# SiLU gate on one core: tiles of 8 rows with two output buffers and a last store in pieces

## The chip, the cores and the metric

The kernel runs on one core of a Trainium2 chip. A core has a matrix engine (not used here), VectorE (DVE), ScalarE (ACT), GpSimd (POOL) and SyncE (SP), an on-chip memory of 128 partitions (SBUF), and 16 DMA engines that move data between SBUF and the chip's main memory (HBM). Here SP issues the loads and ACT the stores; each of the two has a DMA queue of its own, and both queues are served by the same 16 DMA engines. The metric is device time in microseconds (us), the median of several runs; lower is better.

## The reference

The input has 32 x 512 = 16,384 rows of 2,048 floats. The first half of a row goes through SiLU and is multiplied by the second half.

```python
def reference(x: np.ndarray) -> np.ndarray:
    half_dim = x.shape[-1] // 2
    x1, x2 = (x[..., :half_dim].copy(), x[..., half_dim:].copy())
    silu_x1 = x1 * (1 / (1 + np.exp(-x1)))
    return (silu_x1 * x2).astype(np.float32)
```

So 134.2 MB are read and 67.1 MB are written, and nothing is used twice.

## The kernel before

The rows are cut into tiles. A tile with K rows per partition takes 128 x K consecutive rows of the input; partition p holds rows pK to pK+K-1, so each partition is filled from one contiguous run of K x 8 KiB and gives back one contiguous run of K x 4 KiB. The plan (lines 34 to 50) is one tile with K = 4, twenty with K = 6, and one with K = 4: 22 tiles.

The loop at line 54 goes over the tiles in order. For each it takes an input buffer `xt` from `in_pool` (2 buffers of 48 KiB per partition), issues the load on SP (line 59), takes an output buffer `ot` from `out_pool` (4 buffers of 24 KiB), and then works through the tile in pieces of KC = 2 rows: ACT computes SiLU of the first halves into `ot` (line 64), DVE multiplies `ot` in place by the second halves (line 69). When all pieces are done, ACT issues one store of the whole tile (line 74).

The order of work follows from the queues and the buffers. SP holds only loads; the load of tile i+2 waits until DVE has read tile i, since it takes the same buffer. ACT's queue is: the tile's activations, then its store, which waits for DVE's last multiplication, then the next tile's activations. The first activation of a tile waits for the load, and for the store that last used its `ot` buffer (four tiles back). The framework inserts these waits.

Of the kernel before, what the change touches and what calls it, by code (L numbers as in the profile page):

```python
# [1 line left out]

# [4 lines left out]


@with_exitstack
def kernel(  # L10
    ctx: ExitStack,
    tc: tile.TileContext,
    x: bass.AP,
    out: bass.AP,
):
    nc = tc.nc
    P = nc.NUM_PARTITIONS

    x_flat = x.flatten_outer_dims()
    out_flat = out.flatten_outer_dims()  # L20

    num_rows, in_cols = x_flat.shape
    half = in_cols // 2
    dt = x_flat.dtype

    K_MAIN = 6
    K_EDGE = 4
    KC = 2

    in_pool = ctx.enter_context(tc.tile_pool(name="in_pool", bufs=2))  # L30
    out_pool = ctx.enter_context(tc.tile_pool(name="out_pool", bufs=4))

    rows_per_part_total = num_rows // P
    rem = rows_per_part_total - 2 * K_EDGE
    if rem > 0 and rem % K_MAIN == 0:
        plan_k = [K_EDGE] + [K_MAIN] * (rem // K_MAIN) + [K_EDGE]
    else:
        plan_k = []
        rem = rows_per_part_total
        while rem > 0:  # L40
            k = min(K_MAIN, rem)
            plan_k.append(k)
            rem -= k

    plan = []
    row = 0
    for k in plan_k:
        plan.append((row, k))
        row += P * k
    assert row == num_rows  # L50

    KT = max(K_MAIN, K_EDGE)

    for bi, (row0, K) in enumerate(plan):
        xv = x_flat[row0:row0 + P * K].rearrange("(p k) d -> p k d", k=K)
        ov = out_flat[row0:row0 + P * K].rearrange("(p k) d -> p k d", k=K)

        xt = in_pool.tile([P, KT, in_cols], dt, name="xt")
        nc.sync.dma_start(out=xt[:, :K, :], in_=xv)  # L59

        ot = out_pool.tile([P, KT, half], dt, name="ot")
        for c in range(0, K, KC):
            ce = min(c + KC, K)
            nc.scalar.activation(  # L64
                out=ot[:, c:ce, :],
                in_=xt[:, c:ce, :half],
                func=mybir.ActivationFunctionType.Silu,
            )
            nc.vector.tensor_mul(  # L69
                out=ot[:, c:ce, :],  # L70
                in0=ot[:, c:ce, :],
                in1=xt[:, c:ce, half:],
            )
        nc.scalar.dma_start(out=ov, in_=ot[:, :K, :])


# [1 line left out]
_INS = ['x']  # L78
_OUTS = [((32, 512, 1024), 'float32')]


# [23 lines left out]
```

## Time and profile before

| | |
|---|---|
| median of 3 runs | 474.58 us (474.44 to 474.65) |
| span of the profiled execution | 473.1 us |
| ACT activation, 128x2048 | x64, mean 1899 ns |
| DVE multiplication, 128x2048 | x64, mean 2287 ns |
| load of 6 rows per partition | 6144 KB, 34.8 us from issue to landing |
| store of 6 rows per partition | 3072 KB, 27.8 us from issue to landing |
| load / store of 4 rows per partition | 20.7 / 15.4 us from issue to landing |

The span runs from the first to the last instruction of the profiled execution; the measured time also holds what lies around it. Engine rows give the busy time and its share of the span. A digit row cuts the span into 40 equal slices and gives the busy share of each in tenths. For the DMA queues the page gives packets, megabytes and the time that the packets took as a share of 16 engines' span; q1 is the queue of SP's loads, q10 that of ACT's stores. "Landing" is the moment when a DMA's completion reaches the waiting engine.

### The profile page before, as it was taken

To read this page: it belongs to the slowest core of one execution; us is meant where nothing else is said; L and a number is where in the kernel's file an instruction comes from. 1 tells how busy PE (TensorE), PEld (TensorE's weight loads), DVE (VectorE), ACT (ScalarE), POOL (GpSimd) and SP (SyncE) were. 2 spreads that over 40 slices of the span, in tenths; PEclk is the share of its full clock that TensorE was granted. 3 is DMA by queue.
4 is the path that set the end of the run, shared out by engine and by line. 5 is a ranking of instruction groups with operands and counts; after the bars stand their busy time and mean duration, and the time that the engine had idled before them with its cause. 6 is when DMAs were issued, how large, how long until landed. Compare 5 with 4: busy or idle time off the path is not lost.

```text
span 473.1 us, 296 instructions
## 1 busy us (share of the span) xinstructions
DVE 142.9 (30%) x64; ACT 118.9 (25%) x65; POOL 0.2 (0%) x4
## 2 busy tenths in 40 slices
DVE  0323505050514324050505142231505050513323
ACT  1340404041231404040413214040404042231411
POOL 0000000000000000000000000000000000000000
DMA  8999999999999999999999999999999999999995
GB/s 355 449 398 424 432 430 455 420 428 451 414 432 441 432 443 432 416 434 447 426 428 457 418 435 436 443 432 424 432 443 418 438 453 411 451 432 418 433 420 244
DMA packets 6338, 201.35 MB, mean 426 GB/s; under 512 B 704, under 2 KB 704, under 8 KB 704
## 3 DMA queue, kind: packets, MB, share of 16 engines
q1 hardware_dynamic: 3168, 134.22, 65.9%
q10 hardware_dynamic: 3168, 67.11, 33.0%
q14 instruction: 2, 0.02, 0.0%
HBM read 134.22 MB, written 67.11 MB: 426 GB/s over the span
## 4 chain that ended last, share of the span: by engine, by line
DMA 78%; DVE 14%; ACT 4%; issue 1%; DVEq 0%; SPq 0%; ACTq 0%
DMA xt<-in_x_dram 78%; DVE ot L69 14%; ACT ot L64 4%; DVEq L100 0%; SPq L59 0%; ACTq L64 0%
## 5 line engine op out<-in xcount | busy, mean ns | idle before, releaser
L69 DVE TENSOR_TENSOR ot<-ot,xt 128x2048 f32<-128x2048 f32 x64 | 142.9, 2287 | 322.8 <-ACT ot L64 322.8
L64 ACT ACTIVATE ot<-xt 128x2048 f32<-128x2048 f32 x64 | 117.6, 1899 | 343.4 <-DMA xt<-in_x_dram 343.4
L64 ACT ACT_TABLE_LOAD x1 | 1.3, 1283 | 0.7 <-PEq L89 0.7
L89 POOL MEMSET const-bfloat16-1.0<- 128x1 bf16 x1 | 0.1, 103 | 0.0
L89 POOL MEMSET const-uint8-127<- 128x1 uint8 x1 | 0.1, 103 | 0.0
L89 POOL MEMSET const-float32-1.0<- 128x1 f32 x1 | 0.1, 100 | 0.0
L89 POOL MEMSET const-float32-0.0<- 128x1 f32 x1 | 0.1, 99 | 0.2 <-issue 0.2
## 6 DMA issues: line engine op xcount, KB each, us to landing
xt<-in_x_dram SPq DMA_DIRECT2D x20, 6144.0 KB, 34.8
out_dram<-ot ACTq DMA_DIRECT2D x20, 3072.0 KB, 27.8
xt<-in_x_dram SPq DMA_DIRECT2D x2, 4096.0 KB, 20.7
out_dram<-ot ACTq DMA_DIRECT2D x2, 2048.0 KB, 15.4
```

The source lines that it names most:

```text
L64: nc.scalar.activation(out=ot[:, c:ce, :], in_=xt[:, c:ce, :half], func=mybir.ActivationFunctionType.Silu,)
L69: nc.vector.tensor_mul(out=ot[:, c:ce, :], in0=ot[:, c:ce, :], in1=xt[:, c:ce, half:],)
L89: nc = _bacc.Bacc("TRN2", target_bir_lowering=False, num_devices=1)
```

## The change

Every tile has 8 rows per partition: 16 equal tiles, loads of 64 KiB per partition and stores of 32 KiB. The input pool keeps two buffers (now of 64 KiB), the output pool has two (of 32 KiB) instead of four, so the SBUF in use is 192 KiB per partition in both kernels. The first two loads are issued ahead of the loop, and the load of tile i+2 is issued at the end of tile i. Of the last tile each piece of 2 rows is stored on its own, right after its multiplication in the program's text. The chunk size of the compute stays at 2 rows, SP issues the loads and ACT the stores as before.

```diff
-    K_MAIN = 6
-    K_EDGE = 4
+    K = 8
     KC = 2
+    n_tiles = num_rows // (P * K)
+    assert n_tiles * P * K == num_rows
 
     in_pool = ctx.enter_context(tc.tile_pool(name="in_pool", bufs=2))
-    out_pool = ctx.enter_context(tc.tile_pool(name="out_pool", bufs=4))
+    out_pool = ctx.enter_context(tc.tile_pool(name="out_pool", bufs=2))
...
+    xv = x_flat.rearrange("(n p k) d -> n p k d", p=P, k=K)
+    ov = out_flat.rearrange("(n p k) d -> n p k d", p=P, k=K)
...
+    def load(i):
+        xt = in_pool.tile([P, K, in_cols], dt, name="xt")
+        nc.sync.dma_start(out=xt, in_=xv[i])
+        loaded[i] = xt
...
+    load(0)
+    load(1)
+    for i in range(n_tiles):
+        xt = loaded.pop(i)
+        last = i == n_tiles - 1
+        ot = out_pool.tile([P, K, half], dt, name="ot")
         for c in range(0, K, KC):
-            ce = min(c + KC, K)
+            ce = c + KC
...
+            if last:
+                nc.scalar.dma_start(out=ov[i][:, c:ce, :], in_=ot[:, c:ce, :])
-        nc.scalar.dma_start(out=ov, in_=ot[:, :K, :])
+        if not last:
+            nc.scalar.dma_start(out=ov[i], in_=ot)
+        if i + 2 < n_tiles:
+            load(i + 2)
```

More of the change, by code (lines that the diff above doesn't have):

```diff
@@ L24 @@
     dt = x_flat.dtype
-    K_MAIN = 6
-    K_EDGE = 4
+    K = 8
     KC = 2
+    n_tiles = num_rows // (P * K)
+    assert n_tiles * P * K == num_rows
     in_pool = ctx.enter_context(tc.tile_pool(name="in_pool", bufs=2))
-    out_pool = ctx.enter_context(tc.tile_pool(name="out_pool", bufs=4))
[L33 to L61, printed above, removed]
+    out_pool = ctx.enter_context(tc.tile_pool(name="out_pool", bufs=2))
+    xv = x_flat.rearrange("(n p k) d -> n p k d", p=P, k=K)
+    ov = out_flat.rearrange("(n p k) d -> n p k d", p=P, k=K)
+    loaded = {}
+    def load(i):
[8 more added lines that the diff above has]
+        ot = out_pool.tile([P, K, half], dt, name="ot")
         for c in range(0, K, KC):
-            ce = min(c + KC, K)
+            ce = c + KC
             nc.scalar.activation(
```

## The prediction

> **What bounds the kernel now.** I read the busy shares first, then the DMA queues, then the waits, then the chain, and last the windows at the end of the span. From the page:
>
> ```profile
> span 473.1 us, 296 instructions
> DVE 142.9 (30%) x64; ACT 118.9 (25%) x65; POOL 0.2 (0%) x4
> DMA  8999999999999999999999999999999999999995
> q1 hardware_dynamic: 3168, 134.22, 65.9%
> q10 hardware_dynamic: 3168, 67.11, 33.0%
> HBM read 134.22 MB, written 67.11 MB: 426 GB/s over the span
> ```
>
> No compute engine reaches a third. The 16 DMA engines are 9 tenths or more busy in every slice but the first and the last; loads (q1) and stores (q10) together fill 98.9% of them. So the time is bytes over rate, plus what the engines stand idle at both ends. The waits say the same: ACT waits for loads in every tile, and no row has it waiting for a store.
>
> ```profile
> ACT ot L64 <- DMA xt<-in_x_dram: 343.4, 22, 16.8
> DVE ot L69 <- ACT ot L64: 322.8, 22, 15.6
> ```
>
> The chain of waits shows the cadence: two tiles from 116.28 to 159.88 us, 43.55 on average, so 21.77 us for a tile of 6 rows (6.29 MB in, 3.15 MB out): 433.5 GB/s. The end, by timeline and then by windows (columns: stretch, length, busy DVE, ACT and POOL, clock, DMA share, GB/s):
>
> ```profile
> 459.29 3.71 ACT L64 ACTIVATE ot<-xt 128x2048 f32<-128x2048 f32 x2 [10.47 <-DMA xt<-in_x_dram]
> 461.23 4.49 DVE L69 TENSOR_TENSOR ot<-ot,xt 128x2048 f32<-128x2048 f32 x2 [9.29 <-ACT ot L64]
> 465.76 0.34 ACTq L74 DMA_DIRECT2D out_dram<-ot  x1
> ```
> ```profile
> 462.00:463.00 1.00, 1.00 (x1) 0.99 (x1) 0.00 (x0) 1.00 0.97 418
> 463.00:464.00 1.00, 1.00 (x2) 0.00 (x0) 0.00 (x0) 1.00 0.12 49
> 464.00:465.00 1.00, 1.00 (x1) 0.00 (x0) 0.00 (x0) 1.00 0.00 0
> 465.00:466.00 1.00, 0.72 (x1) 0.00 (x0) 0.00 (x0) 1.00 0.00 0
> 466.00:467.00 1.00, 0.00 (x0) 0.00 (x0) 0.00 (x0) 1.00 0.62 262
> ```
>
> The last load lands at 459.26; the engines finish the older store at about 463.1 (3.85 us of backlog), then stand idle until about 466.4, since the last store waits for the whole tile. That hole of 3.3 us is the only one that a schedule of this kind can win back. After it come 4.8 us of store and 1.9 us to the end of the span (471.2 to 473.1).
>
> **What the Trainium skill says.** "DMA: Bandwidth & Descriptors", Where 436 GB/s comes from: 16 SBUF ports give 435 GB/s. The trace agrees, 433.5: only 0.4% is left for a better stream. The same page, Queues, rings and completion order: each DMA engine takes turns between the queues packet by packet. The page of the profile fits: 3168 packets are 22 DMAs x 144, that is 16 engines x (8 runs + 1 semaphore), so one run of one partition, 48 KiB or 24 KiB, is one packet, and with both queues filled the bytes go 2 to 1. The same page, Latency and other measured facts: HBM rows at a pitch of 512 KiB gave 207 GB/s where 214 is full, 3% less, and larger powers of two far less. No run here shows such a pitch; I use it for a rival.
>
> **The change part by part.**
>
> Unit: one 8-row load is 8.39 MB / 433.5 = 19.35 us of all engines, one store 9.68, one cycle 29.0.
>
> Issues. SP has 16 instead of 22 issues of 0.33 us, ACT 19 instead of 22 of 0.36, beside full queues: 0. Loads are issued at the end of tile i instead of the start of tile i+2, but SP carries nothing else and waits for the same thing, DVE's last read of tile i. Cost 0.
>
> Load slack. A 6-row tile takes 8.65 us from first activation to store issue (443.31 to 451.97), an 8-row tile one more multiplication, 11.0. The load of i+2 is issued 11.0 after load i landed, while load i+1 needs 29.0: 18 us of slack (13 before). Cost 0; without that cover each microsecond late would be paid 16 times.
>
> Output buffers 4 to 2. The activation of tile i newly waits for store i-2. Replay, with T(i) the landing of load i: load 1 runs alone until store 0 starts at T(0)+12.0 (11.0 and about 1 us to start), has 7.35 left, gets two thirds, so T(1) = T(0)+23.0; store 0 has moved 3.68 and has 6.0 left, done at T(1)+18. From there both queues are always filled, so T(i+1) = T(i)+29.0, and store i-2 lands at about T(i)-10. Behind a late wait stand ACT's whole queue and then DVE, but the 18 us above cover that too. Cost 0. The old kernel replayed likewise (6-row load 14.5, store 7.25, stores issued 8.65 after a landing): store 1 starts 9.7 after T(1), load 2 lands at T(1)+18.9 with 3.05 of store 1 moved, and 4.2 is left; that backlog is carried on to the last landing. Measured there: 3.85. So I trust the replay to about half a microsecond.
>
> Packets. A run grows to 64 and 32 KiB; packets fall by a quarter. If all of the 0.4% under the ceiling were per packet, a quarter of 1.8 us returns: 0 to -0.45. I take 0, because the ceiling itself may not be exact.
>
> Start. First compute moves from 13.1 to about 22.8, but load 1 is queued behind load 0: engines stay busy. The first two slices miss little more than start-up. Cost 0; bounds -0.5 to +0.5, since a dip at 24 to 28 us, when the first store joins, is unexplained.
>
> End. At T(15) store 14 has 6.0 left. In the built program ACT's order for the last tile is three activations, three stores, the fourth activation, the fourth store. ACT is free at T(15)+5.5 (three activations, 5.51), piece 0 is issued then and its bytes start 0.6 later, as before (465.76 to 466.4): 6.1, just as the backlog ends: 0.1 idle. Each piece is 2.42 us. Pieces 1 and 2 are issued at 6.5 and 8.8 and queue behind piece 0: busy to 13.4. The fourth activation is held behind piece 2's store and its wait for DVE: 9.2 to 11.1, multiplication to 13.4, issue at 13.4, bytes from 14.05: 0.7 idle. Last bytes at 16.5, end of span 1.9 later, T(15)+18.4.
>
> Sum: bytes equal, idle at the end 0.8 instead of 3.3: -2.5. A quarter of a microsecond is taken off for the doubt in the backlog (if it ends 1 us sooner, idle is 1.8 and the gain 1.5): -2.3. Span 470.8. The profiled run's own whole time is not given; the median 474.58 lies 1.5 above its span, and I leave that as it is: 472.3 us.
>
> **The rivals.**
>
> Slower by the stream's rate: partition starts in HBM now lie 64 KiB apart for loads and 32 KiB for stores, powers of two, where 48 and 24 were not, and engines that run in step might meet in the same part of HBM. The place is the 440 us of steady cadence; it decides from 0.5% on (2.3 of 464). Bounds 0 (the old stream is at the ceiling) and 3% (the skill's 512 KiB row, 14 us). An estimate between, 0.8%, is +3.7, less 2.3: 476.0. Against it: the old kernel's last load has a pitch of 32 KiB, and while it runs the rate is no lower:
>
> ```profile
> 445.00:450.00 5.00, 4.75 (x3) 3.81 (x3) 0.00 (x0) 1.00 1.02 441
> 450.00:455.00 5.00, 1.94 (x1) 0.00 (x0) 0.00 (x0) 1.00 1.08 465
> 455.00:459.00 4.00, 0.00 (x0) 0.00 (x0) 0.00 (x0) 1.00 0.93 401
> ```
>
> Slower by arbitration: if a run of 64 KiB goes as two packets of 32, turns are one to one and stores drain at half the rate instead of a third. Then T(1) = T(0)+26.7 with 2.3 of store 0 left, store 1 is all out by T(2) = T(1)+31.4, and so on in turn; T(15) finds 2.3 of backlog, the engines idle from there to 6.1, and 0.7 later: 4.5 against 3.3, +1.2, 475.8. For it: no run of 64 KiB has been seen here. Against: 48 KiB goes as one.
>
> No change: the backlog at T(15) is some 2 us shorter than replayed (stores favoured when the first joins): idle from T(15)+4.0 to 6.1 and 0.7 later, 2.8 instead of 3.3, -0.5, and the dip at the start grows by 0.2 with the larger first tile: 474.3.
>
> Faster still: packets give their 0.45 and the backlog covers the whole start of the pieces: 471.6. It belongs to the forecast's own range.
>
> **How the numbers follow.** Forecast (end hole filled) 0.60, own range 471.4 to 473.5, all of it faster; no change 0.13; rate 0.15, slower; arbitration 0.12, of which two thirds are slower by over 0.2% (0.95 us, what a measurement here can tell from no change) and one third not. Faster 0.60, same 0.17, slower 0.23. The range: the forecast's low end to the rate rival's middle, 471.3 to 476.0, which leaves out half of the rate case and a little of the forecast.
>
> **What would show it.** Right: a cadence of 29.0 us, DMA share 1.0 and 433 GB/s in the middle, no idle microsecond after the last load but one of about 0.7 before the fourth piece, and 18.4 us from the last load's landing to the end. Packets: 144 for each load; 272 would speak for arbitration, and idle engines from 2 to 6 us after the last landing with it. A cadence of 29.2 or more would speak for the rate. A row in which ACT waits for a store would show the buffers to be short. If the span falls though the hole stays, my account of the end is wrong.

## The result and the profile after

| | before | after |
|---|---|---|
| median | 474.55 us (474.44 to 474.65, 4 runs) | 471.88 us (471.59 to 472.29, 4 runs) |
| ratio | | 0.9943, 95% interval 0.9928 to 0.9957 |
| span of the profiled execution | 473.1 us | 470.1 us |
| landing of the last load | 459.29 us | 452.05 us |
| from there to the end of the span | 13.8 us | 18.05 us |

The changed kernel is 2.7 us faster. The two spans differ by 3.0, since the profiled execution of the kernel before was a little slower than its median: in every run for which both are known, the time is 1.7 to 1.8 us above the span, so a span of 473.1 belongs to a run of about 474.9. The page of the changed kernel:

```profile
span 470.1 us, 267 instructions
DVE 142.4 (30%) x64; ACT 118.3 (25%) x65; POOL 0.2 (0%) x4
DMA  8999999999999999999999999999999999999998
q1 hardware_dynamic: 2304, 134.22, 66.2%
q10 hardware_dynamic: 2736, 67.11, 33.1%
out_dram<-ot ACTq DMA_DIRECT2D x15, 4096.0 KB, 39.7
```

Compare the digit row with that of before: nothing differs but the last slice, 8 instead of 5. The loads' packets are 2304 / 16 = 144 for each load, so a run of 64 KiB went as one packet. Between the second and the last landing (the first activation of each tile in the timeline; 45.89 and 452.05 below) 14 tiles take 406.2 us, 29.0 each, and 12.58 MB in 29.0 us is 434 GB/s, the rate of before to within about a tenth of a percent. That tenth turns out to count; it is taken up in the section on the prediction.

The waits of the changed kernel (who waited for whom; us in total, times, longest):

```profile
ACT ot L56 <- DMA xt<-in_x_dram: 340.4, 16, 21.9
DVE ot L61 <- ACT ot L56: 322.9, 17, 24.7
ACT ot L56 <- DVE ot L61: 3.5, 1, 3.5
```

No row has ACT waiting for a store: two output buffers are enough. The third row is new. It is the last tile's fourth activation, held behind the third piece's store. Two parts of the timeline, the second landing and the end (start, duration, engine, what):

```profile
45.89 5.51 ACT L56 ACTIVATE ot<-xt 128x2048 f32<-128x2048 f32 x3 [15.84 <-DMA xt<-in_x_dram]
...
452.05 5.51 ACT L56 ACTIVATE ot<-xt 128x2048 f32<-128x2048 f32 x3 [21.65 <-DMA xt<-in_x_dram]
456.32 4.74 ACTq L67 DMA_DIRECT2D out_dram<-ot  x3
461.11 1.91 ACT L56 ACTIVATE ot<-xt 128x2048 f32<-128x2048 f32 x1 [3.54 <-DVE ot L61]
465.37 0.34 ACTq L67 DMA_DIRECT2D out_dram<-ot  x1
```

And by windows of it (stretch, length, busy DVE, ACT, POOL, clock, DMA share, GB/s):

```profile
448.00:449.00 1.00, 0.00 (x0) 0.00 (x0) 0.00 (x0) 1.00 0.00 0
...
457.00:458.00 1.00, 1.00 (x1) 0.56 (x1) 0.00 (x0) 1.00 0.54 229
458.00:459.00 1.00, 1.00 (x2) 0.00 (x0) 0.00 (x0) 1.00 0.93 393
...
464.00:465.00 1.00, 1.00 (x1) 0.00 (x0) 0.00 (x0) 1.00 0.95 401
465.00:466.00 1.00, 0.34 (x1) 0.00 (x0) 0.00 (x0) 1.00 0.24 98
466.00:467.00 1.00, 0.00 (x0) 0.00 (x0) 0.00 (x0) 1.00 0.94 393
```

The last two columns need care. The view books a packet, with all its bytes and its whole duration, in the window in which the packet starts. A packet of 32 KiB lasts 1.2 us here and one of 64 KiB 2.4 us, so a single microsecond can show too little or too much: the window at 448 shows nothing at all, though all 16 engines were busy through it. Where this text says "by packets", the figure is therefore worked out from the start and the duration of every packet in the trace, as a mean over the 16 engines.

By packets, the engines stood idle for 3.3 us between the older store and the last one in the kernel before. Now the older store ends 6.0 us after the last landing and each engine goes straight on to the first piece; the thin window at 457 is only such an effect of booking. One hole is left, before the fourth piece: 0.9 us by packets, 0.8 by the windows.

### The profile page after: what moved, and what is told of

Read it like the earlier page. It is cut to its first block, busy times and chain, and to the rows that moved or that the text cites. A ratio compares the mean times of both kernels' runs of the same rounds, so it can differ in the third digit from the quotient of the medians.

```text
span 470.1 us, 267 instructions
## 1 busy us (share of the span) xinstructions
DVE 142.4 (30%) x64; ACT 118.3 (25%) x65; POOL 0.2 (0%) x4
## 3 DMA queue, kind: packets, MB, share of 16 engines
q1 hardware_dynamic: 2304, 134.22, 66.2%
## 4 chain that ended last, share of the span: by engine, by line
DMA 80%; DVE 15%; ACT 4%; issue 0%; ACTq 0%; SPq 0%
DMA xt<-in_x_dram 80%; DVE ot L61 15%; ACT ot L56 4%; SPq L45 0%; ACTq L67 0%; ACTq L56 0%
## 6 DMA issues: line engine op xcount, KB each, us to landing
out_dram<-ot ACTq DMA_DIRECT2D x15, 4096.0 KB, 39.7
```

## The experiments

Each was timed beside the kernel before, on the same chip; that kernel's median was 474.55 or 474.56 each time, as in the table above, so the experiments can be set beside the changed kernel's 471.88 as well.

**1. The last store in pieces, on the old tiles.**

```diff
-        nc.scalar.dma_start(out=ov, in_=ot[:, :K, :])
+            if bi == len(plan) - 1:
+                nc.scalar.dma_start(out=ov[:, c:ce, :], in_=ot[:, c:ce, :])
+        if bi < len(plan) - 1:
+            nc.scalar.dma_start(out=ov, in_=ot[:, :K, :])
```

> The old tiles of 4, 6 and 6 rows; only the last store goes in two pieces of 2 rows. Theory of the end hole: the backlog ends 3.85 us after the last landing, the first piece's bytes start at 4.85, the second queues behind it; the idle engines shrink from 3.3 to about 1.0 us, so 2.3 us faster than before: 472.3. Theory of the stream (the gain comes from larger runs and fewer packets): as before, 474.5.

Measured: 472.42 us (472.35 to 472.54, 5 runs), ratio 0.9955 (0.9943 to 0.9967). Windows:

```profile
462.00:463.00 1.00, 1.00 (x1) 0.67 (x1) 0.00 (x0) 1.00 0.91 393
463.00:464.00 1.00, 1.00 (x2) 0.00 (x0) 0.00 (x0) 1.00 0.07 25
464.00:465.00 1.00, 1.00 (x1) 0.00 (x0) 0.00 (x0) 1.00 0.94 393
```

One thin microsecond where there were 3.3 of idle time (0.8 by packets). Pieces alone, on the old tiles, bring 2.1 of the 2.7 us.

**2. The new tiles with the last store whole.**

```diff
-            if last:
-                nc.scalar.dma_start(out=ov[i][:, c:ce, :], in_=ot[:, c:ce, :])
-        if not last:
-            nc.scalar.dma_start(out=ov[i], in_=ot)
+        nc.scalar.dma_start(out=ov[i], in_=ot)
```

> The new tiles of 8 rows; only the last store is one store of the whole tile again. Theory of the end hole: the store is issued 11.0 us after the last landing and its bytes start at 11.6, while the backlog ends at 6.0: 5.6 us idle instead of 0.7, and 4.8 us more from the last landing to the end than the changed kernel: 476.7, slower than before by about 2. Theory of the stream: near the changed kernel, at most 1 us above it, and faster than before.

Measured: 476.75 us (476.64 to 477.31, 5 runs), ratio 1.0049 (1.0037 to 1.0061). Windows:

```profile
457.00:458.00 1.00, 1.00 (x1) 1.00 (x2) 0.00 (x0) 1.00 0.23 98
458.00:459.00 1.00, 1.00 (x2) 1.00 (x2) 0.00 (x0) 1.00 0.08 33
459.00:460.00 1.00, 1.00 (x1) 0.87 (x1) 0.00 (x0) 1.00 0.00 0
...
463.00:464.00 1.00, 0.40 (x1) 0.00 (x0) 0.00 (x0) 1.00 0.00 0
464.00:465.00 1.00, 0.00 (x0) 0.00 (x0) 0.00 (x0) 1.00 1.22 524
```

The hole has grown to more than six microseconds (6.3 by packets), since the last tile has 8 rows to compute instead of 4. So the change is two changes of opposite sign: the larger tiles, with the loads issued ahead and two output buffers, alone cost 2.2 us (476.75 against 474.55), and on them the pieces bring 4.9 (476.75 to 471.88).

**3. The changed kernel with loads in runs of 32 KiB.** The input buffer gets a gap in the middle, so that the DMA cannot join the two halves of a partition's data; compute reads the same values (the rest of the edit, where the activation and the multiplication step over the gap, is left out here).

```diff
-        xt = in_pool.tile([P, K, in_cols], dt, name="xt")
-        nc.sync.dma_start(out=xt, in_=xv[i])
+        xt = in_pool.tile([P, 2, 4 * in_cols + 16], dt, name="xt")
+        nc.sync.dma_start(
+            out=xt[:, :, :4 * in_cols],
+            in_=xv[i].rearrange("p (h k) d -> p h (k d)", h=2),
+        )
...
```

> The changed kernel with each load as two runs of 32 KiB per partition in one DMA (a gap in the input buffer keeps them apart). Theory of turns per packet with a carried backlog: loads and stores take turns one to one, stores drain faster, the backlog at the last landing falls from 6.0 to about 2.3 us and the engines idle some 3.7 us more at the end: 475.6, with the landing of the last load that much later and the time from it to the end as before, 18.1 us. Rival, that bytes or DMAs and not packets are shared out: 471.9 as the changed kernel.

Measured: 477.4 us, ratio 1.0052 (1.004 to 1.0064). From its page and its windows:

```profile
q1 hardware_dynamic: 4352, 134.22, 65.7%
out_dram<-ot ACTq DMA_DIRECT2D x15, 4096.0 KB, 23.4
```
```profile
458.00:459.00 1.00, 0.00 (x0) 1.00 (x1) 0.00 (x0) 1.00 0.46 197
459.00:460.00 1.00, 0.22 (x1) 1.00 (x2) 0.00 (x0) 1.00 0.16 66
460.00:461.00 1.00, 1.00 (x1) 1.00 (x1) 0.00 (x0) 1.00 0.00 0
461.00:462.00 1.00, 1.00 (x2) 1.00 (x2) 0.00 (x0) 1.00 0.00 0
462.00:463.00 1.00, 1.00 (x2) 1.00 (x1) 0.00 (x0) 1.00 0.16 66
```

The loads now have 272 packets each, the same bytes in the same number of DMAs, and a store lands 23.4 us after its issue instead of 39.7. Followed from the end of one packet to the start of the next, the packets of the two queues alternate one by one wherever both have work, in the changed kernel and here. So the two queues take turns by packet, and a smaller load packet gives the stores more.

Stores that drain early leave nothing to cover the last tile's compute. By packets the older store ends 1.6 us after the last landing, where 2.3 were expected, and the first piece's bytes start 5.1 us after it, at 463.0. That is 3.6 us of idle time, and another 1.5 follow before the fourth piece.

The direction is as expected, the size is not: 5.5 us above the changed kernel instead of 3.7. By packets the end is idle 4.2 us longer than in the changed kernel, the start 0.5, and the stream itself is slower, 433.1 GB/s against 433.8 between 60 and 440 us, which is 0.7 us over the whole. The expectation had only the first of the three. Landings alternate between about 34 and 24 us, as turns of one to one with a store that runs dry make them, up to the eleventh tile; then one pair takes 60.0 instead of 58.1. Five runs lie at 477.3 to 477.7, one at 475.53, close to the expected 475.6. That one has no trace, and what shifts the alternation was not found.

**4 and 5. The hole before the fourth piece.** First all four pieces go from SP, whose queue is empty by then; then the first two from ACT and the last two from SP.

```diff
-                nc.scalar.dma_start(out=ov[i][:, c:ce, :], in_=ot[:, c:ce, :])
+                nc.sync.dma_start(out=ov[i][:, c:ce, :], in_=ot[:, c:ce, :])
```

> The changed kernel with the four last stores issued by SP, whose queue is empty by then, so ACT's fourth activation is not held behind the third piece's store. Theory of the end hole: the fourth piece is issued 11.1 us after the last landing, before the engines run dry, and the 0.7 us hole goes: 471.2. Rival: the fourth piece is not what ends last, or the pieces lose as much by sharing turns with the backlog: 471.9.

```diff
-                nc.scalar.dma_start(out=ov[i][:, c:ce, :], in_=ot[:, c:ce, :])
+                eng = nc.scalar if c < 4 else nc.sync
+                eng.dma_start(out=ov[i][:, c:ce, :], in_=ot[:, c:ce, :])
```

> The changed kernel with the first two of the last four pieces issued by ACT and the last two by SP, so that the fourth activation is not held behind the third piece's store and SP's queue is started while ACT's still has bytes. Theory, that the hole of 0.7 us before the fourth piece was worth 0.7 us and that the version with all four pieces on SP lost as much where SP's queue, empty by then, started up beside the end of the backlog: 471.2. Rival, that the end of the kernel is bound elsewhere: 471.9.

Measured: 471.88 us (471.56 to 472.13, 5 runs) and 472.12 us (471.64 to 472.57, 5 runs). Neither gains. Windows of the first:

```profile
457.00:458.00 1.00, 1.00 (x1) 1.00 (x2) 0.00 (x0) 1.00 0.69 172
458.00:459.00 1.00, 1.00 (x2) 1.00 (x1) 0.00 (x0) 1.00 0.62 156
...
465.00:466.00 1.00, 0.00 (x0) 0.00 (x0) 0.00 (x0) 1.00 1.01 426
```

The hole at 465 is gone. But the packets that start between 457 and 459, the first on SP's queue, run slowly: 172 GB/s at a share of 0.69 is 249 while the engines are busy, and 156 at 0.62 is 252, where the changed kernel has 393 at 0.93, that is 423. By packets this loses about 0.5 us. The second version shows no such dip, at 458 or where SP's pieces come in later, and its hole is gone too:

```profile
458.00:459.00 1.00, 1.00 (x2) 0.00 (x0) 0.00 (x0) 1.00 0.91 385
...
465.00:466.00 1.00, 0.00 (x0) 0.00 (x0) 0.00 (x0) 1.00 0.99 418
466.00:467.00 1.00, 0.00 (x0) 0.00 (x0) 0.00 (x0) 1.00 0.97 410
467.00:468.00 1.00, 0.00 (x0) 0.00 (x0) 0.00 (x0) 1.00 0.68 287
468.00:469.00 1.00, 0.00 (x0) 0.00 (x0) 0.00 (x0) 1.00 0.06 25
```

Yet it gains nothing, and the packets show why: the 16 engines do not run dry together. In this version the older store ends 5.5 to 6.0 us after the last landing on fourteen engines, and at 6.6 and 6.8 on the other two. The four pieces are 32 packets of 0.309 us on an engine, 9.9 us. With no hole each engine runs on to its own end: fourteen are done between 467.5 and 468.0, the last at 468.80 (6.8 + 9.9 = 16.7 us after the landing at 452.16). In the changed kernel every engine has to wait for the fourth piece, the late ones catch up in the hole, and all end between 468.73 and 468.88. So my theory of that hole fell: it can be filled, but then the slowest engine sets the end, and its last byte comes only 0.1 us sooner. Why two engines lag stays open.

**6. Two output buffers on the old kernel.**

```diff
-    out_pool = ctx.enter_context(tc.tile_pool(name="out_pool", bufs=4))
+    out_pool = ctx.enter_context(tc.tile_pool(name="out_pool", bufs=2))
```

> The kernel before with two output buffers instead of four. Theory that the buffers have slack: a store lands about 27.8 us after its issue, 7 us ahead of the landing of the load whose tile wants its buffer, so nothing waits: 474.6 as before. Rival, that the pool of two costs something that the pieces of the changed kernel make up for: slower by 0.5 us or more, with ACT waiting for stores.

Measured: 474.63 us (12 runs), ratio 1.0003 (0.9994 to 1.0011), and ACT waits for no store. Two of the four buffers did nothing.

**7. One output buffer on the changed kernel** (the pool's `bufs=2` becomes `bufs=1`).

> The changed kernel with one output buffer, which takes the cover away: a tile's compute cannot start until the store of the tile before has landed. Theory: load and store then start together after each compute, end together 29.0 us later, and the engines stand idle for the 11.0 us of compute and some 2 us of latency; a cycle of about 42 us instead of 29.0, 660 to 690 us in all. Rival, that the load running ahead covers most of it: a cycle below 33 us, under 540 us.

One run: 677.93 us, span 676.2. Its waits:

```profile
ACT ot L56 <- DMA out_dram<-ot: 525.8, 15, 38.7
ACT ot L56 <- DMA xt<-in_x_dram: 20.6, 1, 20.6
```

The wait for loads has turned into a wait for stores, and a cycle takes 43.6 us (42 expected). So between two buffers and one lies the whole cover, and its loss is paid at every tile.

**8. The changed kernel with an earlier start.**

```diff
+        if i == 0:
+            nc.sync.dma_start(out=xt[:, :4, :], in_=xv[i][:, :4, :])
+            nc.sync.dma_start(out=xt[:, 4:, :], in_=xv[i][:, 4:, :])
+        else:
+            nc.sync.dma_start(out=xt, in_=xv[i])
```

> The changed kernel with the first load as two loads of 4 rows, so that compute starts some 10 us sooner and store 0 is issued 6.5 us after the first tile has landed instead of 11.0. Theory of a backlog that is set at the start and carried to the end: store 0 is further along when load 1 lands, 4.1 us of backlog are carried instead of 6.0, the pieces find an empty queue at the end and the engines idle about 1.9 us more: 473.8, with the time from the last landing to the end unchanged. Rival, that an earlier start is worth something or nothing: 471.9 or lower.

Measured: 474.54 us (474.23 to 475.08, 13 runs), 2.7 us slower than the changed kernel and no faster than before (ratio 0.9999, 0.9991 to 1.0007). Compute starts at 12.78 us instead of 22.75 and store 0 is issued at 28.93 instead of 33.62; load 1 lands 25.5 us after the first tile (25.3 by the replay) instead of 23.1:

```profile
12.78 3.71 ACT L60 ACTIVATE ot<-xt 128x2048 f32<-128x2048 f32 x2 [10.77 <-DMA xt<-in_x_dram]
22.46 3.71 ACT L60 ACTIVATE ot<-xt 128x2048 f32<-128x2048 f32 x2 [5.97 <-DMA xt<-in_x_dram]
28.93 0.38 ACTq L73 DMA_DIRECT2D out_dram<-ot  x1
47.99 3.71 ACT L60 ACTIVATE ot<-xt 128x2048 f32<-128x2048 f32 x2 [21.82 <-DMA xt<-in_x_dram]
```

The end pays for it. The last load lands at 454.54, and:

```profile
457.00:458.00 1.00, 1.00 (x1) 1.00 (x1) 0.00 (x0) 1.00 0.31 131
458.00:459.00 1.00, 1.00 (x2) 1.00 (x2) 0.00 (x0) 1.00 0.01 0
459.00:460.00 1.00, 1.00 (x1) 1.00 (x1) 0.00 (x0) 1.00 0.45 188
```

By packets the backlog ends 3.6 us after the last landing instead of 6.0, and the engines idle 1.6 us before the first piece. They idle again before the fourth, for 1.5 us instead of 0.9: the first three pieces are through sooner, while the fourth is still issued 13.32 us after the landing. From the landing to the end it is 18.2 us, as expected nearly the same as in the changed kernel (18.05); the lost cover shows as a landing that comes 2.5 us later. The second hole is most of what the expectation of 473.8 missed. What was won on stores at the start is missing as cover 430 us later.

## Why the prediction was right

The likeliest case, the end hole filled, is what happened: 472.3 forecast, 471.88 measured, a gain of 2.7 us where 2.3 was forecast. Step by step:

- **Start.** First landing at 22.75 (22.8 forecast), load 1 another 23.1 later (23.0), then cycles of 29.0 (29.0). Cost nothing, as forecast; experiment 8 adds what the step did not see, that the larger first tile gives the backlog.
- **Issues, load slack, output buffers.** All at nothing. By packets the engines are never idle between 5 us and the last landing; for the buffers, the waits of the changed kernel and experiment 6 show it, and experiment 7 shows what the second buffer is worth.
- **Packets.** Taken at 0 out of a possible 0.45, and here the forecast was short. By packets the stream between 60 and 440 us ran at 433.4 GB/s in three traces of the old tiles, at 433.7 to 433.8 in five of the new ones, and at 433.1 with loads in runs of 32 KiB: the fewer the packets, the faster, and 433.4 to 433.8 is about 0.4 us of 464. Old and new tiles also differ in where partitions start in HBM; experiment 3 halves the loads' packets and leaves the addresses in HBM as they are. The 29.0 us of a cycle are too coarse to show this.
- **Rivals.** A run of 64 KiB goes as one packet, so the arbitration rival did not come about; experiment 3 brought it about, and it lies 2.8 us over the kernel before, where the rival had 1.2 (477.4 against 475.8). The rate rival fell with the cadence: 434 GB/s at the new pitch. The rival of no change needed a backlog some 2 us shorter, and it was as replayed. Faster still, 471.6, came nearest: the packets gave most of their 0.45 and the backlog covered the start of the pieces, but the hole before the fourth piece stayed.
- **End.** By packets, 6.0 us of backlog after the last landing (6.0 forecast); fourth activation at 9.06 (9.2), fourth piece issued at 13.32 (13.4), end of span at 18.05 (18.4). Wrong was that piece 0 waits until ACT is free: it was issued 4.27 us after the landing, not 5.5, while the third activation still ran (to 457.56). It cost nothing, as the backlog covered the piece's start; in experiment 3, with no backlog left, bytes start 5.1 us after the landing, not 6.1. Two readings of the windows were off as well, because of how they book packets: bytes start 0.8 to 1.0 us after an issue, not 0.6, and from the last bytes to the end of the span it is 1.4 us before and 1.3 after, not 1.9. In the forecast of the end these two nearly cancel, which is luck.
- **The trust in the replay** rests in part on luck. For the old kernel it has load 2 landing 18.9 us after load 1; measured are 20.3. The first tile's store goes in packets of 16 KiB against 48 KiB of load, so by the prediction's own rule it gets a quarter and not a third, which gives an estimate of 20.3 to 20.5. The last load, with packets of 32 KiB against 24, shifts the shares once more. Redone with both, the backlog comes to about 4.4 us, where the prediction had 4.2 and the three traces of the old tiles show 4.1 to 4.4. The changed kernel has one packet size for loads and one for whole stores, so its replay was not touched.
- **The sum.** By packets the gain of 2.94 us in the two spans is made of 2.36 at the end (3.33 to 0.97 of idle time, counting the engines that end early), 0.48 in the stream and 0.15 behind the last bytes, less 0.05 at the start. The forecast had 2.5 for the end, nothing for the stream, and took a quarter of a microsecond off for doubt. In the medians the gain is 2.7, since the profiled run of before lay some 0.3 us above its median; for the same reason the 1.5 us that were added to the span came out low.

So the mechanism and the sign are shown by experiments 1, 2 and 8. Three numbers place it: pieces on old tiles 472.42, new tiles without pieces 476.75, both 471.88. The 0.5 us that larger tiles add to the pieces do not come from the end: the engines idle there for 0.9 us in experiment 1 and 1.0 in the changed kernel. They match the faster stream, which is the term of the prediction that stood at 0.

## What to carry to other kernels

When the DMA engines are full from start to end, look at what they do after the last load: the time to win is the stretch in which the last tile computes and nothing is left to store. Cut the last store into pieces, and keep enough older stores queued to cover the first piece; a larger tile without the pieces makes that stretch longer. A stream that shares engines carries its backlog from the first tiles to the last, so a change at the start (an earlier first tile) or in the packets (smaller ones for the loads) can be paid for at the end. Before filling a last small hole, see whether the engines run dry together: if one lags, it sets the end. And before reading a hole of a microsecond from a view by windows, ask where the view books a packet that is longer than the window.

## What the runs showed of the hardware

- Two queues on the same DMA engines share them by packet, not by byte or by DMA: the packets alternate one by one, and halving the load's run from 64 to 32 KiB, with bytes and DMAs unchanged, shortened a store's time to landing from 39.7 to 23.4 us.
- The same bytes in fewer packets moved slightly faster: 433.1 GB/s with loads and stores in 32 KiB, 433.4 with 48 and 24 KiB, 433.8 with 64 and 32 KiB.
- ACT's queue issues a DMA while activations ahead of it still run: the first piece's store went out at 456.32 while the third activation ran to 457.56. A later activation, in turn, is held behind a store that waits (3.5 us for the fourth).
- The first pieces on a queue that had run dry were slow in experiment 4: 249 and 252 GB/s while busy in the two microseconds in which SP's queue took over from the older store, where 423 was usual when the pieces followed on the queue in use. In experiment 5, where SP's pieces came in while ACT's were still moving, no such dip is seen. What makes the difference was not found.
- The 16 engines do not finish a store together: in the changed kernel the older store ended between 5.6 and 6.7 us after the last landing, depending on the engine.
